# One hybrid decoder step: inverse square roots by a GpSimd power in place of Newton steps on VectorE, and one column product for the attention norm

## The chip, the cores and the metric

The kernel runs on one core of a Trainium2 chip. The core has five engines that run their own instruction queues in order and wait for each other by semaphores: TensorE (PE in the profile; its weight loads are listed apart as PEld), VectorE (DVE), ScalarE (ACT), GpSimd (POOL) and SyncE (SP), which here issues nearly all DMA transfers. The metric is the device time of one execution in microseconds (us), as the median of several runs; a profile of one execution is read beside it.

## What is computed

One layer of a decoder trunk for a prompt of 1024 tokens and a sample group of 8 sequences with 8 tokens each; both share weights. All arithmetic is 32 bit. Every sub-block stands between root mean square norms, and this case is about those norms.

```python
def rms_norm(x, g):
    xf = x.astype(jnp.float32)
    y = xf * lax.rsqrt(jnp.mean(xf * xf, axis=-1, keepdims=True) + EPS)
    return (y * g.astype(jnp.float32)).astype(x.dtype)

x = x + 0.5 * rms_norm(swiglu(rms_norm(x, norm_ffn1_pre[l]), ...), norm_ffn1_post[l])
h = rms_norm(x, norm_mix_pre[l]);  z = h @ w_in[l] + b_in[l]
a = rms_norm(attend(q, k, v, attn_sinks[l]), attn_out_norm[l])      # window attention, 8 heads
o = rms_norm(hgrn2(hq, hf, hi), hg_out_norm[l]) * silu(hg)          # per head of 128
x = x + rms_norm(concat([a, o]) @ w_out[l], norm_mix_post[l])
x = x + 0.5 * rms_norm(swiglu(rms_norm(x, norm_ffn2_pre[l]), ...), norm_ffn2_post[l])
```

The results are the new x of both groups, the key and value windows and the recurrent states.

## The kernel before

The 1088 tokens are cut into three groups of 320 (two prompt blocks of 128 and the 64 sample tokens), 384 and 384. Matrix products split each operand into a high and a low part and multiply three times (`mm3`, lines 278 to 280; the split is `split`, lines 255 and 256: a cast on ACT and a difference on DVE). The FFN products of groups 1 and 2 use a fast scheme with seven instead of eight block products (`make_ffn`), whose sums and differences lie on DVE and POOL (lines 671, 709, 734 to 738, 755 to 759). Weights come through three raw buffers that SP fills (line 262 and others); a raw buffer is free again when ACT and DVE have split it.

Work that isn't a big matrix product (norms, attention, recurrence) is written as generators. The function `tick()`, called between pieces of the big products, advances each running generator by some steps, and `need()` runs one to its end. What each engine then does in which order isn't this program order: the kernel is built with a scheduler that simulates a timeline and sorts the instructions of every engine by it. So a change of one instruction's engine or length can shift the order on all engines.

An inverse root is made by `rsqrt` (line 238): a first guess from the number's bits (line 241), half of the argument (line 242), and three Newton steps, each of two instructions where the root is one column (lines 245, 249) or three where it has three or four columns (lines 247, 248, 249). All run on DVE, each on the result of the one before. It is called 38 times:

- `bcast_steps` (norms of group 0 in the transposed layout): squares on ACT, a column product with `omean` on PE, root, a diagonal matrix (`dg`), and a product of `ones` with it that spreads the root over the partitions (`rb`, line 341).
- `row_rms` (lines 394, 395) for the norms ahead of a sub-block of groups 1 and 2, `post_n` (lines 417, 418) for those behind one, and `pre_first` (lines 554 to 557) for the first norm of the kernel. Squares are summed by the accumulator of ACT (line 393 and others) in two halves of 512 columns, added, scaled by 1/1024 and raised by EPS on DVE, then rooted; three columns, one for each block of rows. The scalings are lines 446, 479, 561 and 426.
- `finish_attn_t` (line 1087) behind each of the eight attention blocks of the prompt: the square of the block's output (128 partitions, 4 x 128 columns), four column products that add up in one PSUM column (line 1094), scale and EPS (line 1095), root, diagonal (line 1098), product with `ones` (line 1100), copy (line 1102), and the scaling (line 1105). `finish_attn` does the sample tokens.
- `finish_hgrn` (line 1247) behind each of the nine recurrence blocks, four columns (squares line 1252, mean line 1253, scaling line 1255), then transposes (line 1259), a product with the gate (line 1261) and the split of the mixer's output (lines 1067, 1068).
- `each` (line 1641), three times at the very end: the last FFN result of a row block is added up (line 905), its squares summed (line 1645), mean (line 1648), root, two scalings with the residual (line 1652), and the stores (line 1653).

Of the kernel before, what the change touches and what calls it, by code (L numbers as in the profile page):

```python
# [18 lines left out]
P = 128  # L19
# [12 lines left out]
MAGIC = 0x5F3759DF  # L32
# [11 lines left out]
def tile_step(ctx: ExitStack, tc: tile.TileContext, A: dict, O: list):  # L44
# [77 lines left out]
    S.activation(junk[:, :P], ones, AF.Square)  # L122
    cols = cp.tile([P, NROWS], F32, name="cols")
# [114 lines left out]
    def rsqrt(y, x, wk):  # L238

        t, xh = wk  # L240
        V.tensor_scalar(y.bitcast(I32), x.bitcast(I32), -0.5, float(MAGIC), op0=ALU.mult, op1=ALU.add)
        V.tensor_scalar(xh, x, -0.5, None, op0=ALU.mult)
        for _ in range(3):
            if y.shape[-1] == 1:
                V.scalar_tensor_tensor(t, y, xh, y, op0=ALU.mult, op1=ALU.mult)
            else:
                V.tensor_tensor(t, y, y, op=ALU.mult)
                V.tensor_tensor(t, t, xh, op=ALU.mult)
            V.scalar_tensor_tensor(y, t, 1.5, y, op0=ALU.add, op1=ALU.mult)
# [58 lines left out]
    def bcast_steps(part, w, out):  # L308
# [24 lines left out]
        rsqrt(sm[:, 1, 0:nb], sm[:, 0, 0:nb], (sm[:, 2, 0:nb], sm[:, 3, 0:nb]))  # L333
# [73 lines left out]
    def half_n(y, hf, sm, gpost, scale):  # L407
        for i in range(3):
            S.activation(junk, y[hf][:, i], AF.Square, accum_out=sm[:, 0, 4 * hf + i:4 * hf + i + 1])
        g = gain_row(gpost, scale, hf)  # L410
        yield
        for i in range(3):
            V.tensor_tensor(y[hf][:, i], y[hf][:, i], g, op=ALU.mult)
            yield

    def post_n(n, y, sm, xsrc, xdst):
        V.tensor_tensor(sm[:, 0, 0:3], sm[:, 0, 0:3], sm[:, 0, 4:7], op=ALU.add)
        V.tensor_scalar(sm[:, 0, 0:3], sm[:, 0, 0:3], 1.0 / D, EPS, op0=ALU.mult, op1=ALU.add)
        rsqrt(sm[:, 1, 0:3], sm[:, 0, 0:3], (sm[:, 2, 0:3], sm[:, 3, 0:3]))
# [122 lines left out]
    def pre_first(y, gpre, h, wts, part):  # L542
# [8 lines left out]
        for i in range(3):  # L551
            r = rows_of(0, i)
            S.activation(junk[:r], y[0][:r, i], AF.Square, accum_out=sm[:r, 0, i:i + 1])
            V.scalar_tensor_tensor(junk2[:r], y[1][:r, i], 1.0, y[1][:r, i], op0=ALU.mult, op1=ALU.mult,
                                   accum_out=sm[:r, 0, 4 + i:5 + i])
        V.tensor_tensor(sm[:, 0, 0:3], sm[:, 0, 0:3], sm[:, 0, 4:7], op=ALU.add)
        V.tensor_scalar(sm[:, 0, 0:3], sm[:, 0, 0:3], 1.0 / D, EPS, op0=ALU.mult, op1=ALU.add)
        rsqrt(sm[:, 1, 0:3], sm[:, 0, 0:3], (sm[:, 2, 0:3], sm[:, 3, 0:3]))
# [410 lines left out]
    def mixing(tp, h):  # L969
# [100 lines left out]
        def finish_attn(n, o, r, sl):  # L1070
# [4 lines left out]
            rsqrt(sm[:r, 1, 0:1], sm[:r, 0, 0:1], (sm[:r, 2, 0:1], sm[:r, 3, 0:1]))  # L1075
# [11 lines left out]
        def finish_attn_t(n, ob, sl):  # L1087

            sm, sq = small(), t2()
            S.activation(sq, ob, AF.Square)  # L1090
            yield
            bank = axbank("ms")
            for m in range(4):
                PE.matmul(bank[:, P:P + 1], sq[:, m * P:(m + 1) * P], ones[:, 0:1], start=m == 0, stop=m == 3)
            V.tensor_scalar(sm[:, 0, 0:1], bank[:, P:P + 1], 1.0 / 512, EPS, op0=ALU.mult, op1=ALU.add)
            rsqrt(sm[:, 1, 0:1], sm[:, 0, 0:1], (sm[:, 2, 0:1], sm[:, 3, 0:1]))
# [150 lines left out]
        def finish_hgrn(n, bank, r, c0):  # L1247
# [6 lines left out]
            rsqrt(sm[:r, 1, :4], sm[:r, 0, :4], (sm[:r, 2, :4], sm[:r, 3, :4]))  # L1254
# [216 lines left out]
        def w_out_units(n, ys, sums):  # L1471
# [14 lines left out]
            for hf in range(2):  # L1486
# [7 lines left out]
                for i in range(3):  # L1494
                    S.activation(junk, banks[i], AF.Square, accum_out=sm[:, 0, 4 * hf + i:4 * hf + i + 1])
                    V.tensor_tensor(y[hf][:, i], banks[i], g, op=ALU.mult)
# [124 lines left out]
    def ready_half():  # L1621
# [7 lines left out]
        for i in range(3):  # L1629
            S.activation(junk, y[:, i], AF.Square, accum_out=sm[:, 0, i:i + 1])  # L1630
            yield
        V.tensor_scalar(sm[:, 1, 0:3], sm[:, 0, 0:3], 1.0 / D, EPS, op0=ALU.mult, op1=ALU.add)
# [8 lines left out]
    def each(i):  # L1641
        need("half")
        y, sm = f2.ys[2], small()
        x, t = sm[:, 0, 1:2], sm[:, 0, 2:3]
        S.activation(junk, y[0][:, i], AF.Square, accum_out=sm[:, 0, 0:1])
        yg = tmp2("yg")
        V.tensor_tensor(yg, y[0][:, i], tail["gb"][0], op=ALU.mult)
        V.tensor_scalar(x, sm[:, 0, 0:1], 1.0 / D, tail["sm"][:, 1, i:i + 1], op0=ALU.mult, op1=ALU.add)
        rsqrt(sm[:, 1, 0:1], x, (t, sm[:, 0, 3:4]))
# [49 lines left out]
```

## Time and profile before

| | us |
|---|---|
| median of 3 runs | 2049.44 (2048.64 to 2050.24) |
| profiled execution, first to last instruction (its span) | 2045.3 |
| ACT busy in it | 933.5 |
| POOL busy in it | 550.1 |

The page has no separate time for the profiled execution as a whole; its span is 4.1 below the median of the runs. Busy time is the sum over an engine's instructions; matmuls overlap, so a busy TensorE isn't one at its peak. The page's strip of 40 slices shows how full TensorE is, and the clock it is granted, in tenths (9 is 90% or more):

```profile
PE   9999999999999999899999998999999999999998
PEclk9999999999999999799999998999999999999999
```

The slices with an 8 or a 7 are the mixing stage (slices 16 and 24, from 818 and 1227 us) and the end. In the rows of a view, `<-` with an engine, a tile and a line names what an instruction waited for.

### The profile page before, as it was taken

The page shows a single profiled execution, that of the slowest core. Times are in us where ns is not written, and L with a number is a line of the kernel's source. Part 1 is how long each engine was busy: PE and PEld are TensorE (multiplying, and loading weights), DVE is VectorE, ACT ScalarE, POOL GpSimd, SP SyncE. Part 2 cuts the span into 40 slices and gives each one's busy share as a digit, 9 for nine tenths or more (in the row PEclk, how much of TensorE's full clock was granted, in tenths as well). Part 3 has the DMA queues.
Part 4 walks back from the last instruction along what each step waited for, and adds up shares of the span by engine and source line. Part 5 has one row for each costly group of instructions (what it writes and reads, how often), then busy time and mean ns, then how long its engine had stood idle before and what let it go on. Part 6 is the DMA issues. An engine that isn't in the chain of part 4 may idle for free.

```text
span 2045.3 us, 34828 instructions
## 1 busy us (share of the span) xinstructions
PE 2006.7 (98%) x13273; PEld 1856.7 (91%) x13273; DVE 1452.6 (71%) x2493; ACT 933.5 (46%) x1679; POOL 550.1 (27%) x508
## 2 busy tenths in 40 slices
PE   9999999999999999899999998999999999999998
PEld 8999999999998987697898897878999999999886
DVE  5776667885568557777678756766889888655667
ACT  6534333444455445435344444544544444444552
POOL 0013433654113101311113310210046554510201
PEclk9999999999999999799999998999999999999999
DMA  8455445556777545556434243525565556576874
GB/s 254 140 158 169 139 156 164 200 182 219 238 235 213 159 149 171 160 145 184 127 96 138 87 141 94 163 87 184 168 193 200 191 188 209 195 241 222 289 257 136
DMA packets 372368, 360.09 MB, mean 176 GB/s; under 512 B 40590, under 2 KB 294361, under 8 KB 372185
## 3 DMA queue, kind: packets, MB, share of 16 engines
q1 hardware_dynamic: 371401, 356.42, 55.2%
q8 instruction: 104, 1.70, 0.3%
q10 hardware_dynamic: 800, 1.44, 0.2%
q14 instruction: 63, 0.52, 0.1%
HBM read 279.85 MB, written 78.94 MB: 175 GB/s over the span
## 4 chain that ended last, share of the span: by engine, by line
PE 91%; DVE 3%; DMA 3%; ACT 1%; issue 1%; SPq 0%; DVEq 0%; ACTq 0%
PE mm L278 27%; PE mm L279 26%; PE mm L280 26%; PE c L280 1%; PE c L278 1%; PE c L279 1%; PE sc L1127 1%; DMA ar<-fa 1%; PE pv L1176 1%; DMA raw<-in_ffn_w_gu_dram 1%; PE lv L1204 1%; PE pT L1165 1%; PE tr L497 1%; DVE w L256 1%; DMA xt<-in_x_prompt_dram 0%
## 5 line engine op out<-in xcount | busy, mean ns | idle before, releaser
L278 PE MATMUL mm<-h,wsph 128*128 128x320 f32 (+1 forms) x1296 | 414.7, 322 | 3.7 <-ACT sg L632 2.2
L279 PE MATMUL mm<-h,wsph 128*128 128x320 f32 (+1 forms) x1296 | 412.5, 319 | 0.0
L280 PE MATMUL mm<-h,wspl 128*128 128x320 f32 (+1 forms) x1296 | 411.7, 318 | 0.0
L255 ACT CAST wsph<-raw 128x1024 fp32r<-128x1024 f32 x202 | 211.3, 1048 | 293.9 <-PE mm L279 237.1
L256 DVE TENSOR_TENSOR wspl<-raw,wsph 128x1024 fp32r<-128x1024 f32 x202 | 251.0, 1245 | 119.3 <-ACT wsph L255 118.5
L256 DVE TENSOR_TENSOR w<-raw,w 128x512 fp32r<-128x512 f32 (+1 forms) x226 | 250.0, 1110 | 84.9 <-ACT w L255 82.8
L255 ACT CAST w<-raw 128x512 fp32r<-128x512 f32 (+1 forms) x226 | 169.6, 754 | 207.3 <-PE mm L279 109.8
L278 PEld LDWEIGHTS mm<-h,wsph 128*128 128x128 f32 x1296 | 244.6, 189 | 11.0 <-issue 3.1
L280 PEld LDWEIGHTS mm<-h,wspl 128*128 128x128 f32 x1296 | 244.7, 189 | 4.0 <-issue 3.5
L279 PEld LDWEIGHTS mm<-h,wsph 128*128 128x128 f32 x1296 | 245.0, 189 | 3.2 <-issue 2.6
L278 PE MATMUL mm<-h,w 128*128 128x384 f32 x704 | 235.8, 335 | 1.2 <-DVE big L725 1.2
L279 PE MATMUL mm<-h,w 128*128 128x384 f32 x704 | 235.8, 335 | 0.0
L280 PE MATMUL mm<-h,w 128*128 128x384 f32 x704 | 230.5, 335 | 0.0
L279 PE MATMUL mm<-w,h 128*128 128x512 f32 x462 | 181.6, 393 | 0.0
L278 PE MATMUL mm<-w,h 128*128 128x512 f32 x462 | 180.8, 395 | 0.5 <-DVE big L905 0.5
L280 PE MATMUL mm<-w,h 128*128 128x512 f32 x462 | 179.5, 392 | 0.0
L280 PE MATMUL mm<-big,w 128*128 128x384 f32 x528 | 176.8, 335 | 1.5 <-DVE w L256 1.5
L279 PE MATMUL mm<-big,w 128*128 128x384 f32 x528 | 176.7, 335 | 0.0
L278 PE MATMUL mm<-big,w 128*128 128x384 f32 x528 | 176.6, 335 | 0.0
L709 POOL TENSOR_TENSOR big<-big 128x384 f32<-128x384 f32 x88 | 111.7, 1269 | 236.5 <-ACT big L722 116.2
L256 DVE TENSOR_TENSOR w<-t,w 128x512 fp32r<-128x512 f32 x176 | 160.5, 922 | 17.5 <-ACT w L255 17.0
L278 PEld LDWEIGHTS mm<-h,w 128*128 128x128 f32 x704 | 132.2, 188 | 1.6 <-DVE big L725 1.6
(359 smaller groups left out, 3881.2 us busy)
## 6 DMA issues: line engine op xcount, KB each, us to landing
raw<-in_ffn_w_gu_dram SPq DMA_DIRECT2D x156, 512.0 KB
raw<-in_ffn_w_down_dram SPq DMA_DIRECT2D x74, 512.0 KB
raw<-in_w_in_dram SPq DMA_DIRECT2D x54, 512.0 KB
ar<-fa SPq DMA_DIRECT2D x70, 384.0 KB
big<-in_ffn_w_down_dram SPq DMA_DIRECT2D x88, 256.0 KB
fb<-big SPq DMA_DIRECT2D x44, 512.0 KB
raw<-fb SPq DMA_DIRECT2D x40, 512.0 KB
fa<-big SPq DMA_DIRECT2D x22, 768.0 KB
```

The source lines that it names most:

```text
L255: S.copy(hi, src)
L256: (lo_eng or V).tensor_tensor(lo, src, hi.bitcast(F32), op=ALU.subtract)
L278: PE.matmul(out, a[0], b[0], start=first, stop=False, skip_group_check=resume)
L279: PE.matmul(out, a[0], b[1], start=False, stop=False, skip_group_check=resume)
L280: PE.matmul(out, a[1], b[0], start=False, stop=last, skip_group_check=resume)
L497: PE.transpose(bank[:, i * P:(i + 1) * P], y[kh][:, i, k * P:(k + 1) * P], ident)
L709: G.tensor_tensor(e[:, i], e[:, i], e[:, i + 1], op=ALU.mult)
L1127: PE.matmul(banks[g][:, i * 256:i * 256 + wk], zq[64 * g:64 * g + 64, 2 * pr + i, b * P:(b + 1) * P], kx[64 * g:64 * g + 64, k0:k0 + wk], ...
L1165: PE.transpose(bank[:, (i * nk + kb) * P:(i * nk + kb + 1) * P], pt[g][:, i, kb * P:(kb + 1) * P], ident)
L1176: PE.matmul(ob[64 * g:64 * g + 64, pr * 256:pr * 256 + 256], vn[:, vb, g * 64:g * 64 + 64], pT[g][:, :2 * wk].rearrange("p (i k t) -> p k ...
L1204: PE.matmul(b4[cs, a, :32], x[:, a, cs], y[:, a, cs], start=True, stop=True)
```

## The change

`rsqrt` is replaced by `root`: one elementwise power on POOL, with a constant tile `mhalf` of -0.5 as exponent. The scratch columns of the Newton steps go. Where squares are summed by ACT, the factor 1/1024 moves into the activation (its input is scaled by 1/32), so the two halves and EPS are added by one instruction on DVE instead of two. In `finish_attn_t` the squares of the four heads in a row are added first, by two instructions on DVE (256 and 128 columns), and one column product takes the place of four.

```diff
-MAGIC = 0x5F3759DF
+RMS = 1.0 / 32.0
...
+    mhalf = cp.tile([P, 4], F32, name="mhalf")
+    G.memset(mhalf, -0.5)
...
-    def rsqrt(y, x, wk):
-        t, xh = wk
-        V.tensor_scalar(y.bitcast(I32), x.bitcast(I32), -0.5, float(MAGIC), op0=ALU.mult, op1=ALU.add)
-        V.tensor_scalar(xh, x, -0.5, None, op0=ALU.mult)
-        for _ in range(3):
-            if y.shape[-1] == 1:
-                V.scalar_tensor_tensor(t, y, xh, y, op0=ALU.mult, op1=ALU.mult)
-            else:
-                V.tensor_tensor(t, y, y, op=ALU.mult)
-                V.tensor_tensor(t, t, xh, op=ALU.mult)
-            V.scalar_tensor_tensor(y, t, 1.5, y, op0=ALU.add, op1=ALU.mult)
+    def root(y, x):
+        G.tensor_tensor(y, x, mhalf[:y.shape[0], :y.shape[1]], op=ALU.pow)
...
-                S.activation(junk[:r], y[hf][:r, i], AF.Square, accum_out=sm[:r, 0, 4 * hf + i:4 * hf + i + 1])
-        V.tensor_tensor(sm[:, 0, b0:b1], sm[:, 0, b0:b1], sm[:, 0, 4 + b0:4 + b1], op=ALU.add)
-        V.tensor_scalar(sm[:, 0, b0:b1], sm[:, 0, b0:b1], 1.0 / D, EPS, op0=ALU.mult, op1=ALU.add)
-        rsqrt(sm[:, 1, b0:b1], sm[:, 0, b0:b1], (sm[:, 2, b0:b1], sm[:, 3, b0:b1]))
+                S.activation(junk[:r], y[hf][:r, i], AF.Square, scale=RMS,
+                             accum_out=sm[:r, 0, 4 * hf + i:4 * hf + i + 1])
+        V.scalar_tensor_tensor(sm[:, 0, b0:b1], sm[:, 0, b0:b1], EPS, sm[:, 0, 4 + b0:4 + b1],
+                               op0=ALU.add, op1=ALU.add)
+        root(sm[:, 1, b0:b1], sm[:, 0, b0:b1])
...
             S.activation(sq, ob, AF.Square)
+            V.tensor_tensor(sq[:, :256], sq[:, :256], sq[:, 256:], op=ALU.add)
+            V.tensor_tensor(sq[:, :P], sq[:, :P], sq[:, P:256], op=ALU.add)
             yield
             bank = axbank("ms")
-            for m in range(4):
-                PE.matmul(bank[:, P:P + 1], sq[:, m * P:(m + 1) * P], ones[:, 0:1], start=m == 0, stop=m == 3)
+            PE.matmul(bank[:, P:P + 1], sq[:, :P], ones[:, 0:1], start=True, stop=True)
             V.tensor_scalar(sm[:, 0, 0:1], bank[:, P:P + 1], 1.0 / 512, EPS, op0=ALU.mult, op1=ALU.add)
-            rsqrt(sm[:, 1, 0:1], sm[:, 0, 0:1], (sm[:, 2, 0:1], sm[:, 3, 0:1]))
+            root(sm[:, 1, 0:1], sm[:, 0, 0:1])
...
-        V.tensor_scalar(x, sm[:, 0, 0:1], 1.0 / D, tail["sm"][:, 1, i:i + 1], op0=ALU.mult, op1=ALU.add)
-        rsqrt(sm[:, 1, 0:1], x, (t, sm[:, 0, 3:4]))
+        V.tensor_tensor(x, sm[:, 0, 0:1], tail["sm"][:, 1, i:i + 1], op=ALU.add)
+        root(sm[:, 1, 0:1], x)
```

The other places that took a root (`bcast_steps`, `post_n`, `pre_first`, `finish_attn`, `finish_hgrn`) change in the same way. Lines of the new kernel are numbered 8 to 9 lower behind the head of the file: its `root` is line 241, and the lines 905, 1094, 1100 and 1652 of before are 896, 1086, 1092 and 1644.

The scheduler sorts the engines anew. Three places matter in what follows. The first is the end of the program on DVE. Before, the last rows are the two scalings (L1652) of the second row block, then mean and Newton steps of the third, then its scalings:

```order
L1652 SCALAR_TENSOR_TENSOR yg_20369<-yg_20369,sm_20367,big_20244 128x512
L1652 SCALAR_TENSOR_TENSOR big_19629<-big_19629,sm_20367,big_20245 128x512
L1648 TENSOR_SCALAR sm_20406<-sm_20406,sm_20243 128x1
L241 TENSOR_SCALAR sm_20406<-sm_20406 128x1
L242 TENSOR_SCALAR sm_20406<-sm_20406 128x1
L245 SCALAR_TENSOR_TENSOR sm_20406<-sm_20406 128x1
L249 SCALAR_TENSOR_TENSOR sm_20406<-sm_20406 128x1
L245 SCALAR_TENSOR_TENSOR sm_20406<-sm_20406 128x1
L249 SCALAR_TENSOR_TENSOR sm_20406<-sm_20406 128x1
L245 SCALAR_TENSOR_TENSOR sm_20406<-sm_20406 128x1
L249 SCALAR_TENSOR_TENSOR sm_20406<-sm_20406 128x1
L1652 SCALAR_TENSOR_TENSOR yg_20408<-yg_20408,sm_20406,big_20244 128x512
```

In the new program the same place on DVE reads:

```order
L1644 SCALAR_TENSOR_TENSOR yg_20021<-yg_20021,sm_20019,big_19903 128x512
L1644 SCALAR_TENSOR_TENSOR big_19299<-big_19299,sm_20019,big_19904 128x512
L896 TENSOR_TENSOR big_18953<-mm_19866,big_18953 128x512
L1639 TENSOR_TENSOR yg_20053<-big_18953,gb_19896 128x512
L1640 TENSOR_TENSOR sm_20051<-sm_20051,sm_19902 128x1
L1644 SCALAR_TENSOR_TENSOR yg_20053<-yg_20053,sm_20051,big_19903 128x512
```

The second row block's scalings now stand ahead of the third's sum (L896), and one addition stands between the sum of squares and the third's scalings.

The second place is PE in the second attention block of group 0, from its column product (`ms` from `ones` and the squares) to the product with the diagonal (`ms` from the tile and `ones`). Before, these rows followed the column product, and the diagonal's product (L1100) came thirteen rows after the last of them:

```order
L1094 MATMUL ms_8420<-ones,t_1173_8333 128x1 x4
L1228 MATMUL l_1187_8435<-t_1112_7926,t_1113_7927 64x64 x4
L454 MATMUL tr_8486<-ident,big_5759 128x128 x3
L454 MATMUL tr_8492<-ident,big_5759 128x128 x3
L278 MATMUL mm_8667<-h_8482,wsph_8663 128x384
L1277 MATMUL kT_8498<-ident,t_1113_7927 128x128 x4
L279 MATMUL mm_8667<-h_8484,wsph_8663 128x384
L280 MATMUL mm_8667<-h_8482,wspl_8664 128x384
L278 MATMUL mm_8667<-h_8482,wsph_8663 128x384
```

In the new program:

```order
L1086 MATMUL ms_8331<-ones,t_1173_8242 128x1
L1220 MATMUL l_1187_8336<-t_1112_7857,t_1113_7858 64x64 x4
L446 MATMUL tr_8387<-ident,big_5728 128x128 x3
L1092 MATMUL ms_8331<-t_1173_8242,ones 128x128
L446 MATMUL tr_8393<-ident,big_5728 128x128 x3
```

One column product stands where four stood, and only two rows are left between it and the diagonal's product.

The third place is POOL around the same block's power (`sm_8241`), in the new program; before, the rows without `mhalf` stood there, in nearly the same order:

```order
L1233 TENSOR_TENSOR t_1113_7858<-t_1113_7858,t_1114_7859 128x32x8
L1233 TENSOR_TENSOR t_1113_7858<-t_1113_7858,t_1114_7859 128x16x16
L1226 COPY At_7862<-cm_7864 32x4x32 x4
L1233 TENSOR_TENSOR t_1113_7858<-t_1113_7858,t_1114_7859 128x8x32
L241 TENSOR_TENSOR sm_8241<-sm_8241,mhalf 128x1
L1233 TENSOR_TENSOR t_1113_7858<-t_1113_7858,t_1114_7859 128x4x64
L1187 MEMSET At_8656 128x512
L241 TENSOR_TENSOR sm_8539<-sm_8539,mhalf 128x4
L241 TENSOR_TENSOR sm_8180<-sm_8180,mhalf 128x3
```

The power is queued among the key factors of the recurrence (L1241 before, L1233 now), each of which waits for a matmul of its level.

More of the change, by code (lines that the diff above doesn't have):

```diff
@@ L408, in half_n @@
         for i in range(3):
-            S.activation(junk, y[hf][:, i], AF.Square, accum_out=sm[:, 0, 4 * hf + i:4 * hf + i + 1])
+            S.activation(junk, y[hf][:, i], AF.Square, scale=RMS, accum_out=sm[:, 0, 4 * hf + i:4 * hf + i + 1])
         g = gain_row(gpost, scale, hf)
@@ L416, in post_n @@
     def post_n(n, y, sm, xsrc, xdst):
[L417 to L419 removed]
+        V.scalar_tensor_tensor(sm[:, 0, 0:3], sm[:, 0, 0:3], EPS, sm[:, 0, 4:7], op0=ALU.add, op1=ALU.add)
+        root(sm[:, 1, 0:3], sm[:, 0, 0:3])
         for i in range(3):
@@ L1494, in w_out_units @@
                 for i in range(3):
-                    S.activation(junk, banks[i], AF.Square, accum_out=sm[:, 0, 4 * hf + i:4 * hf + i + 1])
+                    S.activation(junk, banks[i], AF.Square, scale=RMS, accum_out=sm[:, 0, 4 * hf + i:4 * hf + i + 1])
                     V.tensor_tensor(y[hf][:, i], banks[i], g, op=ALU.mult)
@@ L1629, in ready_half @@
         for i in range(3):
-            S.activation(junk, y[:, i], AF.Square, accum_out=sm[:, 0, i:i + 1])
+            S.activation(junk, y[:, i], AF.Square, scale=RMS, accum_out=sm[:, 0, i:i + 1])
             yield
-        V.tensor_scalar(sm[:, 1, 0:3], sm[:, 0, 0:3], 1.0 / D, EPS, op0=ALU.mult, op1=ALU.add)
+        V.tensor_scalar(sm[:, 1, 0:3], sm[:, 0, 0:3], EPS, None, op0=ALU.add)
         for i in range(3):
```

19 lines of the change are left out of this document (9 added, 10 removed).

## The prediction, made before the changed kernel ran

> **What bounds the kernel now.** I read the page's span, its busy shares and the line of its chain by engine first: they say which engine a saving must reach.
>
> ```profile
> span 2045.3 us, 34828 instructions
> PE 2006.7 (98%) x13273; PEld 1856.7 (91%) x13273; DVE 1452.6 (71%) x2493; ACT 933.5 (46%) x1679; POOL 550.1 (27%) x508
> PE 91%; DVE 3%; DMA 3%; ACT 1%; issue 1%; SPq 0%; DVEq 0%; ACTq 0%
> ```
>
> TensorE is busy for 2006.7 of 2045.3 us and carries 91% of the chain that ended last. So work taken off VectorE (DVE) is worth nothing by itself. The change can earn only in three ways: TensorE instructions that go, the 38.6 us in which TensorE stands, and the clock it is granted. The second view is the table of stretches, ten microseconds each, where TensorE stands (columns: length, then busy time of PE, PEld, DVE, ACT, POOL, then the granted clock, DMA share, GB/s).
>
> ```profile
> 840.00:850.00 10.00, 6.60 (x61) 5.35 (x60) 6.87 (x13) 5.09 (x15) 0.64 (x1) 0.87 0.80 248
> 850.00:860.00 10.00, 7.18 (x70) 4.70 (x70) 7.59 (x26) 5.56 (x13) 3.64 (x6) 0.50 0.70 165
> 860.00:870.00 10.00, 8.10 (x37) 6.61 (x36) 5.73 (x17) 3.12 (x6) 0.61 (x1) 0.61 0.11 30
> 1390.00:1400.00 10.00, 7.75 (x37) 5.36 (x35) 5.86 (x14) 3.33 (x6) 0.00 (x0) 1.00 0.68 196
> ```
>
> From 840 to 870 us TensorE idles 3.40 + 2.82 + 1.90 = 8.1 us, and the clock falls to 0.50: a pile-up that costs twice. The third view, the waits of TensorE by releaser (total, times, longest), says who is late.
>
> ```profile
> PE tr L574 <- DVE big L561: 2.4, 1, 2.4
> PE kT L1277 <- DVE h L459: 1.9, 1, 1.9
> PE lv L1204 <- DVE sm L247: 1.7, 1, 1.7
> PE mm L278 <- ACT h L1067: 1.4, 1, 1.4
> PE sc L1127 <- DVE st L1295: 1.3, 1, 1.3
> ```
>
> Each of these five has Newton steps in front of it on DVE: the head of the kernel (L574), the pile-up (L1277, L1204), the end of the last HGRN block (L1067) and a state update (L1295).
>
> **What is removed and added.** The groups by line give the Newton steps.
>
> ```profile
> L249 DVE SCALAR_TENSOR_TENSOR sm<-sm 128x3 f32<-128x3 f32 (+4 forms) x114 | 19.3, 170 | 2.9
> L248 DVE TENSOR_TENSOR sm<-sm 128x3 f32<-128x3 f32 (+2 forms) x78 | 13.6, 174 | 2.0
> L247 DVE TENSOR_TENSOR sm<-sm 128x3 f32<-128x3 f32 (+2 forms) x78 | 13.1, 168 | 1.3
> L245 DVE SCALAR_TENSOR_TENSOR sm<-sm 128x1 f32<-128x1 f32 (+1 forms) x36 | 8.3, 233 | 0.9
> L241 DVE TENSOR_SCALAR sm<-sm 128x3 int32<-128x3 int32 (+4 forms) x38 | 6.4, 168 | 0.6
> L242 DVE TENSOR_SCALAR sm<-sm 128x3 f32<-128x3 f32 (+4 forms) x38 | 5.8, 154 | 0.0
> L1239 DVE TENSOR_TENSOR t<-t,t 128x256 f32<-128x256 f32 x47 | 26.6, 566 | 7.6 <-PE l L1228 7.4
> ```
>
> 38 roots cost 19.3 + 13.6 + 13.1 + 8.3 + 6.4 + 5.8 = 66.5 us of DVE. Against that stand 16 additions of squares in the eight attention blocks, at most 0.57 us each by the last row, 9 us. About 57 us of DVE go, nearly all of them beside matmuls, so I count them only where a wait above has them in its chain.
>
> **Term 1, the column products.** The chain in order of time shows the eight matmul instructions of one block's sum of squares (four products, two passes each).
>
> ```profile
> 1369.12 0.79 PE ms L1094 x8
> ```
>
> That is 0.10 us each. Six of eight go in each of eight blocks: 48 x 0.099 = 4.7 us of a saturated engine. One block's products lie in the pile-up, beside waits, so I take seven eighths, **-4.1** (bounds 0, if waits refill it, and -4.7).
>
> **What one power costs.** No row shows it. The nearest rows are GpSimd's (POOL) elementwise operations:
>
> ```profile
> L1212 POOL TENSOR_TENSOR t<-t 128x4 f32<-128x4 f32 x8 | 1.6, 203 | 0.5
> L1212 POOL TENSOR_TENSOR t<-t 128x32 f32<-128x32 f32 x9 | 6.1, 680 | 0.7
> L755 POOL TENSOR_TENSOR big<-big 128x512 f32<-128x512 f32 x22 | 33.0, 1498 | 325.9 <-DMA big<-in_ffn_w_down_dram 325.9
> 112.80 2.00 POOL L755 TENSOR_TENSOR big<-big 128x512 f32<-128x512 f32 x1 [110.50 <-DMA big<-in_ffn_w_down_dram]
> ```
>
> A product of the same size is 0.20 us, the low end; the longest row here, 2.00 us, is the high end. A power is many operations on each element; I take the 128x32 product, eight times the elements, **0.7 us**, and 0.1 us for each hand-over between engines, an estimate (at 11.24 us, below, an ACT operation starts within 0.05 us of the DVE step it waits for).
>
> **Term 2, the tail.** Timeline of the last row block:
>
> ```profile
> 2037.67 0.19 ACT L1645 ACTIVATION_READ_ACCUMULATOR junk<-big 128x1 f32 x1
> 2039.01 0.21 DVE L1648 TENSOR_SCALAR sm<-sm,sm 128x1 f32<-128x1 f32 x1
> 2040.85 0.75 DVE L1652 SCALAR_TENSOR_TENSOR yg<-yg,sm,big 128x512 f32<-128x512 f32 x1
> ```
>
> Nothing is left to hide behind here. The sum is there at 2037.86, but DVE first does the previous block's two scalings, then 1.84 us of sum and Newton steps. In the new order the previous scalings stand ahead of the last L905 (shown above), and no other work stands on POOL. So: sum 2037.9 to 2038.1, hand-over, power 0.7, hand-over, scaling at 2039.0 instead of 2040.85: **-1.9**. With a power of 0.2 us -2.3; of 2.0 us -0.6.
>
> **Term 3, the head.** Timeline of DVE before the first scaling, then the chain and TensorE's timeline later on:
>
> ```profile
> 8.87 0.16 DVE L556 TENSOR_TENSOR sm<-sm 128x3 f32<-128x3 f32 x1
> 11.24 0.88 DVE L561 TENSOR_SCALAR big<-big,sm 128x512 f32<-128x512 f32 x2
> 17.03 6.91 DMA raw<-in_ffn_w_gu_dram
> 34.35 0.41 PE L278 MATMUL mm<-h,wsph 128*128 128x320 f32 x1 [0.91 <-ACT sg L632]
> ```
>
> 2.37 us from sum to scaling become 0.2 + 0.1 + 0.7 + 0.1 = 1.1: the first transposes come 1.3 us earlier. Whether that lasts depends on what is late next: the fourth weight tile (asked for at 17.03 behind twelve loads of x on SP; in the new order behind nine) and the Silu at 34 us, on ACT, which has other work. I keep **-0.8** (0 to -1.8).
>
> **Term 4, the mixing stage.** The last HGRN block, on DVE:
>
> ```profile
> 1388.66 0.17 DVE L1253 TENSOR_SCALAR sm<-sm 128x4 f32<-128x4 f32 x1 [1.93 <-ACT t L1252]
> 1394.01 0.69 DVE L1255 TENSOR_TENSOR t<-av,sm 128x512 f32<-128x512 f32 x1
> ```
>
> 5.35 us between the mean and its use, since two weight differences (1.2 us each) and a state update are sorted in between; a power would need about 1.1 us. The 1.4 us wait at L1067 goes and part of the others; with 1.3 us at L1295 and some 2 us in the pile-up (its transfers, gain rows and x tiles, stay late) I estimate -4.7. Against it stand new waits. In the second attention block the diagonal product L1100 now follows the column product at a distance of four 64x64 products and three transposes:
>
> ```profile
> 1249.90 0.61 PE l L1228 x8
> 881.41 0.66 PE tr L454 x6
> L1095 DVE TENSOR_SCALAR sm<-ms x8: 146/152/159, 793.1 to 1369.9; 128x1 f32<-128x1 f32 x8
> L1098 DVE TENSOR_SCALAR t<-ident,sm x8: 267/285/288, 798.6 to 1372.8; 128x128 f32<-128x128 f32 x8
> ```
>
> That is 0.61 + 0.66 = 1.3 us, and it needs 0.15 + 0.1 + 0.7 + 0.1 + 0.29 plus about 0.5 behind a weight difference that DVE does in between: a wait of some 0.6 us. POOL is in order: if the power stands behind a product that waits for a matmul, both wait; I give that 0.9 us over all blocks. Together **-3.2**, with bounds +14 (below) and -15 (the pile-up gone: 8.1 us idle, and 7.18 x 0.50 + 8.10 x 0.39 = 6.8 us of clock).
>
> **Sum.** -4.1 - 1.9 - 0.8 - 3.2 = -10.0 us: a span of 2035.3. The median of the runs, 2049.44, lies 4.1 above the profiled span, which I keep: **2039.5 us**.
>
> On the clock: it fell to 0.50 here though TensorE's longest single wait there was 1.9 us. [...]
>
> **Rivals.**
>
> - *The saving is refilled* (2047, chance 0.12). TensorE reaches the same data and buffers sooner and waits there. For it: the late transfers in 840 to 870 don't depend on roots. Only the tail stays, -1.9. Against: the products lie in stretches where TensorE is 10.00 busy.
> - *A second pile-up* (2053, chance 0.09). Orders on all engines are rebuilt, and roots now go DVE, POOL, DVE in the middle of the mixing stage. If POOL's queue makes several diagonals late at once, TensorE idles 6.2 us within 20 (as from 840 to 860), the clock halves, and the price is that of the present pile-up, 8.1 + 6.8, some +14 on the forecast. It decides once a power with its queueing takes about 3 us in two neighbouring blocks. For it: the 1.3 us distance. Against: in six of the eight blocks 25 to 35 rows of matmuls stand between the two products.
> [...]
> - *The pile-up dissolves* (2030, chance 0.13). The x tiles of that stage are asked for behind one load of w_in in the new SP order, not three; if that and the freed DVE end the waits from 840 to 870, another 8 to 10 us go.
>
> **How the numbers follow.** The forecast (2033 to 2045) has 0.62. Range 2029 to 2050: down to the dissolved pile-up, up past the refilled case; what is left out is the second pile-up and the far end of the dissolved one. A measurement of this kernel can tell about 0.2%, 4.1 us. Faster by more than that: 0.62 + 0.13 = 0.75. Within it: 0.12 + 0.04 = 0.16. Slower: 0.09.
>
> **What would show it.** L1094's successor has 16 matmuls instead of 64. A power of 0.2 to 2.0 us, 38 of them on POOL. DVE near 1396 us busy, PE near 2000. L561 starts near 10 us and the tail's first scaling 1.2 us after its sum of squares. TensorE's idle time in 840 to 870 at or under 8 us. Wrong if a power takes over 2 us, if waits of PE on L1100's or L1259's inputs exceed 3 us in total, or if the clock falls below 0.8 in a stretch that is at 1.00 now.

## The result, and the profile after

The changed kernel takes **2025.4 us** (median of 4 runs, 2020.42 to 2027.24) against 2049.6 before: a ratio of 0.988, 95% interval 0.9866 to 0.9894. That is 24 us less, where 10 were forecast, and below the range's lower end of 2029.0. Here and below a median leaves out three slow runs: one of e7 (2179.8 us, granted clock 0.846) and two of the kernel before (2456.9 at 0.749 beside e17, 3940.2 beside e9 to e12).

The page after, first its span, busy times and chain:

```profile
span 2025.1 us, 34383 instructions
PE 1996.3 (99%) x13225; PEld 1847.8 (91%) x13225; DVE 1398.9 (69%) x2115; ACT 933.8 (46%) x1679; POOL 577.8 (29%) x547
PE 91%; DMA 3%; DVE 2%; issue 1%; ACT 1%; POOL 0%; SPq 0%; DVEq 0%; POOLq 0%; ACTq 0%
```

TensorE stands for 2025.1 - 1996.3 = 28.8 us instead of 38.6, and is busy for 10.4 us less. VectorE has 53.7 us less to do. Where the time went shows when the same split of a weight tile starts on ACT in both traces (line 255 before, 247 after); the last column takes the row above off:

| the same split, or the end | before | after | moved | in this stage |
|---|---|---|---|---|
| before the mixing stage | 712.3 | 711.2 | -1.1 | -1.1 (head) |
| behind the pile-up | 890.0 | 879.7 | -10.2 | -9.1 |
| | 1199.4 | 1185.0 | -14.4 | -4.1 |
| end of the mixing stage | 1444.7 | 1426.2 | -18.5 | -4.1 |
| last split of all | 2022.0 | 2003.5 | -18.5 | 0 |
| span | 2045.3 | 2025.1 | -20.2 | -1.7 (tail) |

Head and tail came near the forecast (-0.8 and -1.9). The mixing stage gave 17.3 us, of which 9.1 lie at one place, the pile-up of 840 to 870 us. Its stretches after (columns as before; the granted clock is the number behind the brackets):

```profile
840.00:850.00 10.00, 9.33 (x88) 6.56 (x88) 7.93 (x16) 7.60 (x16) 3.45 (x6) 1.00 0.58 140
850.00:860.00 10.00, 6.16 (x35) 5.11 (x36) 7.31 (x17) 3.81 (x11) 3.42 (x5) 0.83 0.75 178
860.00:870.00 10.00, 10.00 (x73) 9.03 (x72) 7.83 (x16) 5.67 (x19) 0.52 (x1) 1.00 0.20 56
```

TensorE idles 0.67 + 3.84 = 4.5 us instead of 8.1. What the granted clock falls short of 1.00, summed over the 30 us, is 1.7 us (0.17 x 10) where it was 10.2 (1.3 + 5.0 + 3.9). Five of the waits of TensorE after (total, times, longest):

```profile
PE mm L270 <- DVE big L1488: 4.3, 2, 3.8
PE l L1220 <- POOL t L1233: 1.9, 1, 1.9
PE tr L446 <- DVE t L1097: 1.8, 1, 1.8
PE pT L1157 <- DVE t L1150: 1.3, 1, 1.3
PE mm L270 <- ACT h L1058: 0.6, 1, 0.6
```

The transposes `pT` of the softmax waited for L1158 before, and the largest row of TensorE's waits was theirs:

```profile
PE pT L1165 <- DVE t L1158: 4.4, 2, 2.5
```

Now it is 1.3 us in one time. The longest wait after, 3.8 us behind L1488, lies at 1256.7 us; before, its counterpart (L1496, at 1270.8) took 1.5. New at 852 us is a wait of 1.9 us for POOL's key factors. The timeline of POOL at that place:

```profile
850.56 1.68 POOL L1233 TENSOR_TENSOR t<-t,t 128x256 f32<-128x256 f32 x1
852.21 0.55 POOL L241 TENSOR_TENSOR sm<-sm,mhalf 128x1 f32<-128x1 f32 x1
```

The power stands behind the key factor, not ahead of it, so it isn't what TensorE waited for; the power itself was held up, for its operand had been there at 850.59. The wait of 1.8 us behind L1097, the scaling by that root, isn't the power's either: the copied root was there at 855.04, and VectorE, which had other work in its order first, began the scaling at 857.74.

What one power takes, the groups by shape:

```profile
L241 POOL TENSOR_TENSOR sm<-sm,mhalf 128x3 f32<-128x3 f32 x17 | 20.0, 1178 | 327.6 <-DVE sm L324 165.9 <-DVE sm L410 102.3 <-DVE sm L387 30.9
L241 POOL TENSOR_TENSOR sm<-sm,mhalf 128x4 f32<-128x4 f32 x8 | 8.6, 1076 | 35.6 <-DVE sm L1245 30.7 <-DVE sm L410 5.0
L241 POOL TENSOR_TENSOR sm<-sm,mhalf 128x1 f32<-128x1 f32 x11 | 6.5, 595 | 39.2 <-DVE sm L1087 18.2 <-DVE sm L1640 14.2 <-DVE sm L318 6.8
L1086 PE MATMUL ms<-ones,t 128*128 128x1 f32 x16 | 2.3, 212 | 0.2 <-ACT wsph L247 0.2
```

That is 0.6 us for one column and 1.1 to 1.2 for three or four on the mean (the 38 range from 0.54 to 2.11). The column products fell from 64 to 16 matmuls.

### The profile page after: what moved, and what is told of

It reads as the page before. It is cut to its first block, busy times and chain, and to the rows that moved or that the text cites. A ratio compares the mean times of both kernels' runs of the same rounds, so it can differ in the third digit from the quotient of the medians.

```text
span 2025.1 us, 34383 instructions
## 1 busy us (share of the span) xinstructions
PE 1996.3 (99%) x13225; PEld 1847.8 (91%) x13225; DVE 1398.9 (69%) x2115; ACT 933.8 (46%) x1679; POOL 577.8 (29%) x547
## 4 chain that ended last, share of the span: by engine, by line
PE 91%; DMA 3%; DVE 2%; issue 1%; ACT 1%; POOL 0%; SPq 0%; DVEq 0%; POOLq 0%; ACTq 0%
PE mm L270 27%; PE mm L271 27%; PE mm L272 27%; DMA ar<-fa 1%; PE c L270 1%; PE c L272 1%; PE c L271 1%; PE pv L1168 1%; PE sc L1119 1%; DMA raw<-in_ffn_w_gu_dram 1%; PE lv L1196 1%; PE tr L489 1%; DVE w L248 1%; DMA ar<-act 1%; PE pT L1157 1%
## 5 line engine op out<-in xcount | busy, mean ns | idle before, releaser
L248 DVE TENSOR_TENSOR w<-raw,w 128x512 fp32r<-128x512 f32 (+1 forms) x226 | 246.3, 1094 | 88.2 <-ACT w L247 85.9
L270 PEld LDWEIGHTS mm<-h,wsph 128*128 128x128 f32 x1296 | 244.8, 189 | 12.7 <-issue 5.8
L248 DVE TENSOR_TENSOR w<-t,w 128x512 fp32r<-128x512 f32 x176 | 164.0, 942 | 17.4 <-ACT w L247 17.1
L241 POOL TENSOR_TENSOR sm<-sm,mhalf 128x3 f32<-128x3 f32 (+4 forms) x38 | 36.7, 967 | 404.2 <-DVE sm L324 165.9
```

Of the source, the lines that this page charges most:

```text
L241: G.tensor_tensor(y, x, mhalf[:y.shape[0], :y.shape[1]], op=ALU.pow)
L248: (lo_eng or V).tensor_tensor(lo, src, hi.bitcast(F32), op=ALU.subtract)
L270: PE.matmul(out, a[0], b[0], start=first, stop=False, skip_group_check=resume)
```

## What had happened in the pile-up

Before the experiments, the two traces side by side. Before, VectorE:

```profile
842.40 0.75 DVE L426 SCALAR_TENSOR_TENSOR big<-big,sm,xt 128x512 f32<-128x512 f32 x1 [4.35 <-DMA xt<-in_x_prompt_dram]
...
846.06 0.15 DVE L1149 TENSOR_TENSOR sm<-sm,sm 128x4 f32<-128x4 f32 x1
846.91 1.20 DVE L426 SCALAR_TENSOR_TENSOR big<-big,sm,xt 128x512 f32<-128x512 f32 x1 [0.69 <-DMA xt<-in_x_prompt_dram]
848.04 0.16 DVE L1150 RECIPROCAL sm<-sm 128x4 f32<-128x4 f32 x1
848.24 0.62 DVE L1158 TENSOR_SCALAR t<-t,sm 128x256 f32<-128x256 f32 x2
```

and TensorE, from the last big product of the stage's FFN to the first of the next group (`mm<-h,wsph`):

```profile
844.40 0.39 PE L280 MATMUL mm<-w,h 128*128 128x512 f32 x1
846.29 0.46 PE L1204 MATMUL lv<-t,t 128*32 128x32 f32 x32 [1.50 <-DVE sm L1149]
848.65 1.97 PE L1165 MATMUL pT<-ident,t 128*128 128x128 f32 x8 [1.90 <-DVE t L1158]
852.32 0.66 PE L1204 MATMUL lv<-t,t 128*32 128x32 f32 x32 [1.70 <-DVE sm L247]
...
862.26 0.69 PE L278 MATMUL mm<-h,wsph 128*128 128x384 f32 x1
```

VectorE stands 4.35 us for an x tile (asked for on SP behind three loads of `w_in`), and the last steps of the softmax (L1149, L1150, L1158) are queued behind that scaling. TensorE has no big product left: in its order the last 28 of them stand ahead of `pT`, and none between `pT` and the transposes `tr` that lead to the next group. So from 844.4 to 862.3, 17.9 us, small products wait for one another. The changed kernel, VectorE and TensorE:

```profile
838.45 0.62 DVE L1150 TENSOR_SCALAR t<-t,sm 128x256 f32<-128x256 f32 x2
840.55 0.75 DVE L418 SCALAR_TENSOR_TENSOR big<-big,sm,xt 128x512 f32<-128x512 f32 x1 [1.49 <-DMA xt<-in_x_prompt_dram]
```

```profile
839.89 1.09 PE L1157 MATMUL pT<-ident,t 128*128 128x128 f32 x8
840.74 0.48 PE L270 MATMUL mm<-w,h 128*128 128x512 f32 x1
...
846.11 1.68 PE L1168 MATMUL pv<-t,vn 128*64 128x256 f32 x8 [0.40 <-DVE t L1160]
...
854.97 0.53 PE L270 MATMUL mm<-h,wsph 128*128 128x384 f32 x1
```

Four things differ at once: the x tiles come earlier; the softmax's last steps stand ahead of the last x scaling on VectorE; 24 big products stand behind `pT` in TensorE's order (19 ahead of `pv`, 5 behind it), so that TensorE has work while VectorE copies the transposes for `pv`; and the roots are shorter. The theories, by the letters that the expectations use: **A**, the x tiles' place on SP; **B** or **D**, VectorE's load with Newton steps; **C**, the one column product; **E**, how soon a root is there; **F**, the new order as a whole; **G**, x tiles and the row norm's root are both late, and either one gone is enough; **H**, the row norm's root alone; **J**, remedies that stand in for each other. They were formed one after another, as each run spoke against the one before.

## Experiments

A time is the median, and its difference is to the median of the kernel before in the same session (2047.1 to 2048.5). "At 890" is how much earlier the split at 890 us started, less the head's part (the split at 712); the changed kernel, profiled twice, gave -9.1 and -11.3 there, so 2 us either way are scatter.

**Parts of the change (e1 to e4).** e1 is the kernel before with the new `finish_attn_t` but Newton steps; e2 is the changed kernel with the old column products; e3 and e4 change who takes the root in that function:

```diff
# e3, in the kernel before; e4 the other way round, in the changed kernel
-            rsqrt(sm[:, 1, 0:1], sm[:, 0, 0:1], (sm[:, 2, 0:1], sm[:, 3, 0:1]))
+            root(sm[:, 1, 0:1], sm[:, 0, 0:1])
```

> The kernel before, with the squares of the attention norm added first and one column product; Newton steps stay on VectorE everywhere. All theories: 16 column-product matmuls instead of 64, -4.7 us of TensorE. Theory A (order): the x tiles of the second group still stand on SyncE's queue behind three loads of w_in here, so the pile-up at 840 to 870 us stays (TensorE idle there about 8 us, clock near 0.50): 2045, within 2042 to 2048. Theory B (the roots' load on VectorE made the mixing stage late, place by place): 2045 as well. Theory C (the products, not the roots, opened the pile-up): 2032 to 2037.

> The changed kernel with four column products a block again and no additions of squares; powers on GpSimd everywhere. Theory A (order): the x tiles go ahead of two of the three w_in loads here, no 4.35 us wait of VectorE for an x tile: 2030, within 2027 to 2033. Theory B: 2030 as well. Theory C: the pile-up is back, 2037 to 2042.

> The kernel before, with the power in the eight roots of finish_attn_t alone; 30 roots keep their Newton steps, four column products stay. This alone moves the x tiles ahead of the w_in loads on SyncE's queue, since the tile of squares, from the same pool of eight as the x tiles, is let go earlier in the scheduler's timeline. Theory A (order): most of the gain of the mixing stage comes with it, 7 to 11 us: 2038 to 2043. Theory B (gain in proportion to the VectorE work removed, here 12 of the 57 us): -2 to -4 us, 2045 to 2047.5.

> The changed kernel with Newton steps in the eight roots of finish_attn_t alone; 30 powers and the one column product stay. The x tiles stand behind three w_in loads again. Theory A (order): the pile-up returns, the clock falls to 0.50 for more than 10 us in it: +7 to +11 us, 2032 to 2037. Theory B (in proportion): +2 to +4 us, 2027 to 2029.5.

Measured: e1 2040.11 (-7.0; at 890 -0.8), e2 2023.40 (-23.7; -13.5), e3 2032.46 (-14.6; -9.8), e4 2026.46 (-20.6; -6.2). e1 and e2 came out 2 to 4 us below every theory's range (from 2042 and from 2027). C falls: the products alone leave the pile-up, and without them it is gone. e3, 8 powers of 38, gives more than half of the gain, far beyond B's share. But e4, without those 8, keeps most: A had asked for 2032 or more. Two halves of a change that each give most of the whole point to one obstacle that either removes.

**Load or speed of a root (e6, e7).**

```diff
# e6
-        G.tensor_tensor(y, x, mhalf[:y.shape[0], :y.shape[1]], op=ALU.pow)
+        for _ in range(3):
+            G.tensor_tensor(y, x, mhalf[:y.shape[0], :y.shape[1]], op=ALU.pow)
# e7, behind the one power; d is a small tile that nobody reads
...
+        V.tensor_scalar(d[:r, :c], x, -0.5, None, op0=ALU.mult)
+        for _ in range(8):
+            V.tensor_tensor(d[:r, :c], d[:r, :c], x, op=ALU.max)
```

> The changed kernel with every power written three times into the same place, so a root takes some 2.9 us on GpSimd instead of 0.97, longer than the Newton steps did (ten instructions of 0.17 us), and VectorE has no more work than in the changed kernel. Head and tail lose about 1.9 us each in any case. Theory D (what counts is VectorE's load): about 2025 + 4 = 2029, 2026 to 2032. Theory E (what counts is how soon a root is there): the gain of the mixing stage goes, 2037 to 2046.

> The changed kernel with nine idle instructions on VectorE behind every power (38 x 9 of about 0.165 us, 56 us in all, as many as the change took away), a chain whose result nobody reads; the roots come as early as in the changed kernel but for what queues behind these. Theory D (load): most of the mixing stage's gain goes, 2035 to 2044. Theory E (how soon a root is there): 2025 to 2029.

The groups of e6 and of e7 show that the cost was really put there:

```profile
L242 POOL TENSOR_TENSOR sm<-sm,mhalf 128x3 f32<-128x3 f32 (+4 forms) x114 | 109.1, 957 | 397.7 <-DVE sm L325 164.0 <-DVE sm L411 112.4 <-DVE sm L1246 28.6
```

```profile
L246 DVE TENSOR_TENSOR dum<-dum,sm 128x3 f32<-128x3 f32 (+4 forms) x304 | 50.6, 177 | 4.7
L244 DVE TENSOR_SCALAR dum<-sm 128x3 f32<-128x3 f32 (+4 forms) x38 | 6.0, 161 | 0.6
```

e6 2028.09 (-19.9; at 890 -10.3), e7 2026.79 (-21.2; -7.7). Roots of 2.9 us cost nothing beyond head and tail, and 56.6 us put back on VectorE cost some 4 us at most by the medians: the changed kernel stands at -24.2 and, in e18, at -25.1, and the intervals overlap. So neither the load (D) nor the speed of a root (E) is what the mixing stage gained from. That speaks against the reason that stood behind term 4 of the prediction.

**The x tiles (e5, e9, e10).**

```diff
# e5 in the kernel before, e10 in the changed one
-                nc.sync.dma_start(xt, xsrc[i * P:(i + 1) * P, cs])
+                S.dma_start(xt, xsrc[i * P:(i + 1) * P, cs])
# e9 in the changed one
-                nc.sync.dma_start(xt, xsrc[i * P:(i + 1) * P, cs])
+                tc.keep_in_program_order(nc.sync.dma_start(xt, xsrc[i * P:(i + 1) * P, cs]))
```

> The kernel before, Newton steps and column products as they were; only the x tiles of post_n are asked for on ScalarE's queue instead of SyncE's, so they no longer stand behind loads of w_in. Theory A (the x tiles' place behind w_in makes the pile-up): VectorE's wait of 4.35 us for an x tile goes, TensorE's idle time from 840 to 870 us falls from 8.1 to under 4, the stretch at clock 0.50 from 20.5 to under 11 us; 6 to 10 us faster than before. Theory D (the roots' instructions on VectorE): within 2 us of before.

> The changed kernel with nothing but the x tiles of post_n pinned to program order on SyncE's queue: the sixth of the second group then stands behind four loads of w_in instead of two, the third behind one and the fourth and fifth behind two instead of one each. Powers, products and all instructions stay. Theory A (the x tiles' place makes the pile-up): the last x scaling comes 4 to 6 us later, at 844 to 847 us, TensorE loses 3 to 8 us between 830 and 890: 2028 to 2034. Theory F (the power's new order is better as a whole, wherever the x tiles stand): within 2 us of the changed kernel.

> The changed kernel with the x tiles of post_n asked for on ScalarE's queue, as in e5 for the kernel before. Theory A: little is left to win, since only 2.7 us of VectorE's waits for x tiles are there: 0 to 4 us faster than the changed kernel, 2021 to 2026. Theory F: within 2 us of it; slower than 2028 if ScalarE's queue delays the x tiles of the later groups.

e5 2035.21 (-12.8; at 890 -8.4), which is more than A's 6 to 10; the low clock lasts 10.2 us there, as A had it (under 11). TensorE's order around the pile-up is that of before, row for row in kind and number, and every Newton step is there; only the x tiles come sooner. TensorE in e5:

```profile
844.37 1.10 PE L1165 MATMUL pT<-ident,t 128*128 128x128 f32 x8
848.05 0.46 PE L1204 MATMUL lv<-t,t 128*32 128x32 f32 x32 [2.59 <-DVE sm L248]
...
856.35 0.69 PE L278 MATMUL mm<-h,wsph 128*128 128x384 f32 x1
```

`pT` starts 4.3 us earlier than before and the next group's first product 5.9. So the x tiles alone are a sufficient lever. But the gain of the change doesn't hang on them: e9 (2040.02, -7.6), where x tiles are late again, keeps -11.7 at 890. It loses later, in stages where the other groups' tiles are pinned, above all at a place of the same kind (waits of TensorE in e9 from 1330 to 1360 us):

```profile
PE pT L1157 <- DVE t L1150: 4.9, 1, 4.9
```

There again no big product stands between `pT` and the small products behind it, for 9.6 us. e10: 2024.39 (-23.2; -10.1), not told apart from the changed kernel.

**x tiles against the row norm's root (e13 to e16).** e13 pins the x tiles in the first call of `post_n` alone, e14 puts Newton steps into `row_rms` alone, e15 does both; e16 is the kernel before with the power in `row_rms` alone.

```diff
# e13, e15, in post_n (calls is an empty list set up ahead of it)
+        calls.append(n)
+        pin = len(calls) == 1
...
-                nc.sync.dma_start(xt, xsrc[i * P:(i + 1) * P, cs])
+                ld = nc.sync.dma_start(xt, xsrc[i * P:(i + 1) * P, cs])
+                if pin:
+                    tc.keep_in_program_order(ld)
# e14, e15; e16 the other way round in the kernel before
-        root(sm[:, 1, b0:b1], sm[:, 0, b0:b1])
+        rsqrt(sm[:, 1, b0:b1], sm[:, 0, b0:b1], (sm[:, 2, b0:b1], sm[:, 3, b0:b1]))
```

> The changed kernel with the x tiles pinned to program order in the first call of post_n alone (the stage at 840 us), the later groups free. e9 kept its gain at 890 us although its last x scaling there came at 844.7, and lost 9 us from 1312 to 1389, where the later groups' tiles were pinned too. Theory G (between the last x tile and the first product of the next group two things are late, the x tiles and the row norm's Newton steps behind them, and taking away either brings that product to some 855 us, where TensorE's own order holds it): 2022 to 2029. Theory A (the x tiles' place alone): 2030 to 2035.

> The changed kernel with Newton steps in row_rms alone (the norm between the x tiles and the next group's products); the x tiles stay ahead of the w_in loads. Theory G: one of two late things is back, the first product of the next group still comes by 858: 2024 to 2030. Theory H (the row norm's Newton steps alone made the pile-up): 2032 to 2038.

> The changed kernel with both: Newton steps in row_rms, and the x tiles pinned in the first call of post_n; all other powers, the one column product, head and tail stay. Theory G: the pile-up is back, the stretch of TensorE without a big product between 830 and 880 is longer than 12 us and the first product of the next group later than 858: 6 to 11 us slower than the changed kernel, 2031 to 2037. Theory F (the power's order as a whole): 2023 to 2029.

> The kernel before with the power in row_rms alone; the x tiles stay behind three loads of w_in, four column products and the other Newton steps stay. Theory G: one of two late things gone, the first product of the next group at 855 to 858 instead of 862: 5 to 11 us faster than before, 2037 to 2043. Theory A: within 3 us of before.

e13 2023.95 (-23.6; -12.9), e14 2024.15 (-23.4; -13.3), e15 2027.35 (-20.2; -11.5), e16 2043.44 (-4.1; -0.9). G and H fall: with both late the gain stays, and e16's rows are scaled at 850.6 instead of 855.8, yet its first product still starts at 862.3. A falls too. What e13, e14 and e15 share with the changed kernel is the order, F. VectorE in e13:

```profile
833.76 0.35 DVE L1156 TENSOR_SCALAR t<-t,sm 128x256 f32<-128x256 f32 x1
837.98 1.41 DVE L424 SCALAR_TENSOR_TENSOR big<-big,sm,xt 128x512 f32<-128x512 f32 x2 [3.87 <-DMA xt<-in_x_prompt_dram]
```

The wait for an x tile is nearly as long as before (3.87 us), but the softmax's last step (L1156) has been done ahead of it, TensorE has its transposes by 836.03, and of the 29 big products behind them 20 stand ahead of the next small one. The same wait costs TensorE nothing.

**How far a new order alone moves the time (e8, e11, e12).** e8 has the power only in `pre_first` and `each`; e11 the same instructions as before with `dg` and `rb` in a tile of their own; e12 only the factor moved into the activation.

```diff
# e8, in pre_first and in each
-        rsqrt(sm[:, 1, 0:3], sm[:, 0, 0:3], (sm[:, 2, 0:3], sm[:, 3, 0:3]))
+        root(sm[:, 1, 0:3], sm[:, 0, 0:3])
...
-        rsqrt(sm[:, 1, 0:1], x, (t, sm[:, 0, 3:4]))
+        root(sm[:, 1, 0:1], x)
# e11, in finish_attn_t
-            dg = sq[:, :P]
+            dg = pp.tile([P, P], F32, tag="dgx", bufs=1, name=uid("dgx"))
...
-            rb = sq[:, P:2 * P]
+            rb = dg
# e12, at every sum of squares, Newton steps kept
-            S.activation(junk, y[hf][:, i], AF.Square, accum_out=sm[:, 0, 4 * hf + i:4 * hf + i + 1])
+            S.activation(junk, y[hf][:, i], AF.Square, scale=RMS, accum_out=sm[:, 0, 4 * hf + i:4 * hf + i + 1])
...
-        V.tensor_tensor(sm[:, 0, 0:3], sm[:, 0, 0:3], sm[:, 0, 4:7], op=ALU.add)
-        V.tensor_scalar(sm[:, 0, 0:3], sm[:, 0, 0:3], 1.0 / D, EPS, op0=ALU.mult, op1=ALU.add)
+        V.scalar_tensor_tensor(sm[:, 0, 0:3], sm[:, 0, 0:3], EPS, sm[:, 0, 4:7], op0=ALU.add, op1=ALU.add)
```

> The kernel before with the power only in pre_first and each, 4 of 38 roots: the head and the tail. All theories: the head gives 1.3 us and the tail 1.7 us as in the changed kernel's trace, and the mixing stage nothing but what a new order brings by chance: 3 us faster than before, within 1 to 5.

> The kernel before with the same instructions; only the diagonal of the attention norm and the copy of its product lie in a tile of their own, so that the tile of squares is let go sooner and the scheduler sorts the mixing stage anew. The x tiles stay behind three loads of w_in. A probe of what a new order alone does: theory A says within 3 us of before, 2045 to 2051; more than 5 us either way would say that orders scatter as much as the effects that are tested here.

> The kernel before with the factor 1/1024 moved into the activations and one addition where an addition and a scaling stood, Newton steps and four column products kept. It takes one short instruction of 0.17 us from each chain, and leaves the x tiles behind three loads of w_in. Theory A: the pile-up stays, within 3 us of before, 2045 to 2050. Theory D (VectorE's load): under 1 us faster.

e8 2041.69 (-6.3; at 890 -2.2), e11 2044.34 (-3.3; +1.7), e12 2044.94 (-2.7; -2.2). All three keep the pile-up. e11 does the same work and is 3.3 us faster (ratio 0.9987, 0.9977 to 0.9996), which is what one other order moved by itself; e8's 6.3 is the 3 forecast plus as much again. e11 also refutes a remark in e3's expectation: letting the tile of squares go sooner doesn't move the x tiles.

**Both remedies at once (e17), and the changed kernel again (e18).** e17 is e2 with e5's line.

> The kernel of e2 (powers everywhere, four column products a block) with the x tiles of post_n asked for on ScalarE's queue as in e5: both remedies at once. Theory J (the stretch at 840 to 870 us is covered already, by big products behind the softmax's transposes on TensorE or by x tiles that come early, and a second remedy adds little): within 4 us of e2's 2023.4, 2019 to 2026. Were the two remedies to add up, as e5's 12.8 us on top of e2, 2010 to 2014.

> The changed kernel once more, beside e17 on the same chip, to see how its time stands to that of its variants: 2020 to 2028 as before. Differences under 3 us between it, e2, e13 and e17 are not told apart.

e17 2019.40 (ratio 0.9859, 0.9842 to 0.9877), e18 2023.44 (0.9881, 0.9865 to 0.9896). At 890, -14.2 against e2's -13.5: the remedies stand in for each other and don't add up. e17 is the lowest of all, but its interval overlaps that of the changed kernel.

All kernels by what stands in TensorE's order between `pT` of that block and the transposes `tr` of the next group. The last two columns are the longest stretch of TensorE between two big products there, and how long the granted clock is at 0.50 there:

| big products behind `pT` | kernels | at 890, us | stretch, us | low clock, us |
|---|---|---|---|---|
| 0, x tiles late | before, e1, e8, e11, e12, e16 | +1.7 to -2.2 | 17.1 to 18.2 | 17.1 to 20.5 |
| 0, x tiles early | e5 | -8.4 | 12.7 | 10.2 |
| 10, x tiles late | e4 | -6.2 | 7.1 | 10.2 |
| 16 to 29 | e6, e10, e7, changed (24), e14, e3, e9, e13, e15 | -7.7 to -13.3 | 4.6 to 10.8 | 0 to 10.2 |
| 43 | e2, e17 | -13.5, -14.2 | 5.3, 4.0 | 3.4, 0 |

Among the kernels with x tiles late, those with cover (e4, e9, e13, e15) gain 6.2 to 12.9, and those without gain nothing beyond 2.2. That is as near as the runs come to showing the cause: an order in which big products stand between the softmax's transposes and the small products that need their result. In e9, e13 and e15 the softmax's last steps also stand ahead of the late x scalings on VectorE, so there the two orders aren't told apart. In e4 they stand behind a wait of 5.1 us for an x tile, as in the kernel before (4.35), and `pT` itself waits about as long (2.17 us against 1.90; line numbers are e4's own):

```profile
839.04 2.08 DVE L432 SCALAR_TENSOR_TENSOR big<-big,sm,xt 128x512 f32<-128x512 f32 x3 [5.10 <-DMA xt<-in_x_prompt_dram]
844.02 0.61 DVE L1164 TENSOR_SCALAR t<-t,sm 128x256 f32<-128x256 f32 x2
```

```profile
844.43 1.69 PE L1171 MATMUL pT<-ident,t 128*128 128x128 f32 x8 [2.17 <-DVE t L1164]
845.77 0.78 PE L286 MATMUL mm<-w,h 128*128 128x512 f32 x1
```

So TensorE's order can differ with VectorE's wait in place; but e4 has 30 powers and the one column product as well. No kernel changed that order alone with Newton steps everywhere; this wasn't tried on the chip. Why the scheduler gives it with a power in the attention norm (e3) and not with one in the row norm (e16) stays open.

## Why the prediction was right in part, and where it failed

*Head, -0.8.* The stage gave 1.1. Sum to scaling takes 1.15 us, as worked out (1.1), and the gain lasts to the end of the FFN:

```profile
8.86 0.16 DVE L548 SCALAR_TENSOR_TENSOR sm<-sm 128x3 f32<-128x3 f32 x1 [0.26 <-ACT junk L545]
9.11 0.86 POOL L241 TENSOR_TENSOR sm<-sm,mhalf 128x3 f32<-128x3 f32 x1 [6.81 <-DVE sm L548]
10.01 0.49 DVE L552 TENSOR_SCALAR big<-big,sm 128x512 f32<-128x512 f32 x1 [0.98 <-POOL sm L241]
```

*Tail, -1.9.* It gave 1.7 in the stage. The timeline of the last row block:

```profile
2019.09 0.19 ACT L1637 ACTIVATION_READ_ACCUMULATOR junk<-big 128x1 f32 x1
2019.31 0.16 DVE L1640 TENSOR_TENSOR sm<-sm,sm 128x1 f32<-128x1 f32 x1
2019.55 0.54 POOL L241 TENSOR_TENSOR sm<-sm,mhalf 128x1 f32<-128x1 f32 x1 [3.15 <-DVE sm L1640]
2020.12 0.75 DVE L1644 SCALAR_TENSOR_TENSOR yg<-yg,sm,big 128x512 f32<-128x512 f32 x1 [0.66 <-POOL sm L241]
```

Sum to scaling is 2020.12 - 2019.28 = 0.84 us; the forecast had 1.2. From that scaling to the end it is 5.0 us where it was 4.5, so that 1.9 came near by two misses that cancel.

*One power, 0.7 us with 0.2 to 2.0.* 0.97 on the mean; the longest, 2.11, lies just past the end, and past the 2 us that the prediction set as a sign of being wrong, but it stands at 592.4 us, far from the mixing stage. The 0.04 among the chances stood for a dear first call, which no run shows: the first power took 0.86 us and began 0.09 after its operand.

*Column products, -4.1.* Here the size can't be confirmed as a whole: e1 gives 7.0, and e2, which has the 48 matmuls still, isn't slower than the changed kernel. Between 890 and 1199 us, where TensorE is busy throughout and three of the eight blocks lie, the changed kernel gains 4.1 and e2 1.4. The difference of 2.7 is near the 1.8 that three blocks should give at 0.6, but e11, which has all the products, gains 5.0 there, so one pair of kernels can't tell. The means can, nearly: -3.5 over the eleven traces with one product a block, -1.5 over the nine with four. Elsewhere the size stays open.

*Mixing stage, -3.2.* **This is the step that failed.** With the products it was -7.3 and became -17.3. It added up waits that had Newton steps in front of them, from a list that left out TensorE's largest, the 4.4 us of `pT` (1.9 of them in the pile-up); and it held that in the pile-up "its transfers, gain rows and x tiles, stay late", so that only some 2 us would go there. It gave 9.1. The x tiles didn't stay late, which only the rival said; and where they did (e9, e13, e15) the pile-up went all the same, with the changed order on TensorE and VectorE. I read the new order where I feared a new wait, and not where the old wait was. The count of big products behind `pT`, 0 before and 24 after, could be read without a run. The waits feared in exchange didn't come as such: the product with the diagonal (L1092) never waits long enough to be listed, and POOL's queue held the power of the second block up by 1.6 us (850.59 to 852.21), which no wait of TensorE shows.

*The rivals.* "The pile-up dissolves" had the place and nearly the size, 8 to 10 us more, and got 0.13. Its mechanism, the x tiles, is one that works (e5), but the gain doesn't need it (e9, e13, e15). "A second pile-up" had its point of decision at powers of about 3 us; e6 has them, and shows none.

*The range.* It ended at 2029, though term 4's own lower bound of -15 gave 10 + 12 = 22 us off, 2027.6. A bound that is in the sum should have been in the range. The measured time lies below that too; with the lower bounds of all four terms (4.7 + 2.3 + 1.8 + 15 = 23.8) the sum would be 2025.6.

## What to carry to other kernels

Where a scheduler rebuilds the order, a stall of before isn't priced by the instructions in front of it: look first at what the bounding engine has between two small instructions that depend on each other, in the old order and in the new. Work behind the instruction that waits didn't shorten its wait (in e4 `pT` waits 2.17 us with ten big products behind it); but independent work ahead of that instruction can cover the time in which other engines make its operand (in e13 a wait of VectorE of 3.87 us cost TensorE nothing). When two halves of a change each give most of its gain, suspect that they remove the same obstacle, and don't add them up. And try the same program in another order before a difference of a few us is put down to an operation: here that alone moved 3 us of 2048.

## What the runs showed of the hardware

In the changed kernel's trace a power on GpSimd took 0.55 us at the median for 128x1, 0.86 for 128x3 and 1.02 for 128x4; a product of 128x4 took 0.20 on the mean in the trace of before. Single powers took up to 2.11; why isn't shown.

Between 840 and 870 us the granted clock was at 0.50 for 20.5 us before and for 3.4 in the changed kernel; in e1 and e8 it was 17.1, in e5 10.2, in e6 6.8. No wait of TensorE there was longer than 1.9 us in the kernel before, and the clock was at 0.50 all the same; what brought it down isn't shown. Over the 20 traces the low clock at that place goes with how long TensorE has no big product: 17.1 or 20.5 us where that is 17 to 18 us, at most 10.2 where it is 4 to 13.
